# An order planned with later landings and later hand-overs, attention norms through PSUM, and the modulation's weights in the first ffn

## The chip, the cores and the metric

The kernel runs on one core of a Trainium2 chip. The metric is the device time in microseconds (us) of one execution. Three executions of the kernel before took 1523.7, 1526.34 and 1527.78 us; the median is 1526.34.

The engines are TensorE (PE: matmuls and transposes), VectorE (DVE), ScalarE (ACT), GpSimd (POOL) and SyncE (SP, which issues the loads).

## The reference

256 tokens of width 1024 go through two blocks. The first has two layers, and each layer a mixer and an ffn:

```
h    = rms_norm(x);  proj = h @ w_in[l]
o_a  = ga0*compressed_attn + ga1*selected_attn + ga2*banded_attn(window 512)
o_b  = silu(layer_norm(depthwise_conv31(a * sigmoid(g))))
o_c  = pool_mixer(c_in)
o_d  = banded_attn(window 128, sinks)            # exp(sink - m) joins the denominator
mix  = sum over b of sigmoid(h @ w_gate[l])_b * (o_b @ w_branch[l, b])
x    = x + rms_norm(mix @ w_o[l])
u    = depthwise_conv3(rms_norm(x) @ w_up);  gate, val = split(u)
x    = x + rms_norm((gelu(gate) * val) @ w_down)
```

In the compressed attention, 15 compressed keys for each of two groups, the probabilities are `softmax` over the masked scores, weighted by the gate `ga0`.

The second block takes the result and a condition c. Its modulation is `silu(c) @ w_mod + b_mod` (w_mod is 1024 x 6144), with a second product `silu(c_ctx) @ w_mod[:, :2048]` for a context of 256 tokens that has its own side computation. Shifts, scales and gates from it enter a mixer with attention and a state scan, and a mixture of 16 experts. Nothing in the first block needs the modulation.

## The kernel before

**Where the time goes, in order.** Mixer 0 runs from the start to about 335 us of the profile, ffn 0 to about 525, mixer 1 to about 815, and the rest is ffn 1 and the second block. Each mixer has a head (the in-projections, with the attentions, the 31-tap convolution on VectorE and the pool mixer beside them), then gates and branches (`gate`, `branch`: 16 products whose weights stream in), then w_o and its renorm.

**Matmuls.** Weights are loaded by SP in tiles of 512 KB (`wr_wr`). ACT rounds a tile to the PE's type (`wh_wh`); POOL, and sometimes VectorE, subtracts the two (`wl_wl` = wr - wh, both inputs in SBUF). Activations are split the same way (`hp_hTh`/`hp_hTl`, `bp_brh`/`bp_brl`), and PE does three matmuls for each product. Everything that PE writes, and some small work of the other engines, goes through eight PSUM banks, all named `ps_bank`.

**What sets the order.** The program is first recorded, not issued. A list scheduler (`run`, L374) then places the recorded instructions on the engines by estimated costs (`cost`, L240), hand-over latencies between engines (`lat`, L298) and a model of the DMA queue; `slack` (L327) works out priorities from the result, and `order` (L306) repeats this ten times and keeps the best. `emit` (L540) issues the instructions in that order, so every instruction in the profile has line L540 and is told apart by its names. Each engine executes its own instructions strictly in this order. What VectorE costs, how late a load is taken to land and how late a result is taken to reach another engine thus set what stands before what, and nothing else.

**The modulation** (`modulation`, L1756). w_mod comes in 96 tiles of 128x512 (`wm_wm`, 256 KB, two buffers), in groups of eight. A row of silu(c), 512 wide, is kept in a PSUM bank for a group, and one SCALAR_TENSOR_TENSOR on VectorE multiplies a tile by it and sums along the row. The first sixteen tiles of the order and the last sixteen are multiplied twice, once for c and once for c_ctx (into a scratch `wk_t2k`), and their groups hold two banks. The generator goes on only while `k.m_on` is set: before, from the first gate of a mixer (L1596) to the start of that layer's ffn (L1657), or to `conv_start` (L1456) in a mixer's head. Its results are first used by the second block, which starts with the w_o of layer 1.

**The attentions.** `attn` (L1085) makes scores, their row minimum `mx` (the scores are negated) and the exponentials with their row sums `sm`. `norm` (L1115) turns the sums into weights: with sinks it adds exp(mx - sinks), then takes the reciprocal `w`, multiplied by the gate where there is a weight, all on 8 columns in SBUF. There are 12 calls of it, four with sinks and eight with a weight. `cmp_attn` (L1300) is the compressed attention: two score matmul groups into one bank, mask, maximum, exponential and sum on VectorE and ACT, then reciprocal, weight and the product `wk_t1k`, which PE transposes. It runs beside the gates.

**ffn** (L1648). Four banks (`n.py`) hold the output sums during an ffn. Up-projections of 128x256 pairs take a bank each; `evac` reads it (three-tap convolution, ACT and VectorE), `act` and `sp` use the same bank for gelu and the split into `bp_brh` and `bp_brl`, after which it is free. `renorm` follows each w_o and each ffn: row sums of squares, a Newton iteration on 128x1 columns on VectorE (`wk_sm`, `wk_nw`, `wk_nwy`), the residual, transposes by PE.

## Time and profile before

| | |
|---|---|
| median of three executions | 1526.34 us |
| the profiled execution | 1523.77 us |
| its span, first to last instruction | 1521.6 us |
| mean granted TensorE clock | 0.984 |
| PE busy | 1437.5 us, 94% |
| VectorE, ACT, GpSimd busy | 69%, 65%, 64% |
| read from HBM | 287.13 MB, 189 GB/s over the span |
| w_mod loads issued, by place | 43 before layer 0's w_up, 7 in ffn 0's head, 37 in mixer 1's gates, 9 behind the first w_o load of layer 1 |

A time in the rows is in us from the start of the span. A duration in brackets is the time that the engine was idle before the instruction, with the instruction or load that ended the idle time. The granted clock (PEclk) is a fraction of full speed: 1.00 is 2.4 GHz and 0.50 is 1.2. In the windows an engine's entry is its busy time and its number of instructions.

### The profile page before, as it was taken

How to read it: one execution, taken by the hardware profiler on the slowest of the kernel's cores; microseconds unless marked ns; L12 is line 12 of the kernel's file. 1: busy time of each engine (PE TensorE's matmuls, PEld its weight loads, DVE VectorE, ACT ScalarE, POOL GpSimd, SP SyncE). 2: the span in 40 equal slices, each digit the busy share in tenths (PEclk: the TensorE clock that was granted, in tenths of full speed). 3: DMA queues.
4: the chain of work that ended last, by engine and by line, in shares of the span. 5: the costliest groups of instructions: out<-in, count | busy, mean ns of one | idle time of the engine just before them, and what ended most of it. 6: DMA issues, size and time to landing. Idle time of an engine off the chain costs nothing.

```text
span 1521.6 us, 23981 instructions
## 1 busy us (share of the span) xinstructions
PE 1437.5 (94%) x8276; PEld 1233.2 (81%) x8276; DVE 1050.8 (69%) x2412; ACT 983.9 (65%) x1773; POOL 971.1 (64%) x504
## 2 busy tenths in 40 slices
PE   8989998989999999899999999999999999899995
PEld 6967886769999798788777999999888778777773
DVE  5889765554333669985467843336888886889997
ACT  5878953556555577886356665556567697476773
POOL 6786587848777677947786677777647572332121
PEclk9999999999999999999999999999999999999998
DMA  8555478856555454637786555555534205358982
GB/s 315 167 172 166 143 263 266 271 195 207 183 189 183 133 193 136 204 127 257 256 273 220 190 182 191 182 186 169 158 116 134 88 29 175 112 180 302 343 291 89
DMA packets 91155, 290.35 MB, mean 191 GB/s; under 512 B 11409, under 2 KB 13713, under 8 KB 91026
## 3 DMA queue, kind: packets, MB, share of 16 engines
q1 hardware_dynamic: 91026, 288.74, 57.0%
q8 instruction: 67, 1.10, 0.3%
q14 instruction: 62, 0.51, 0.1%
HBM read 287.13 MB, written 1.05 MB: 189 GB/s over the span
## 4 chain that ended last, share of the span: by engine, by line
PE 70%; DVE 14%; DMA 8%; ACT 5%; issue 2%; POOL 1%; SPq 0%; DVEq 0%; ACTq 0%; POOLq 0%
PE ps_bank L540 70%; DMA wm_wm<-w_mod 7%; DVE wl_wl L540 3%; DVE wk_t2k L540 3%; DVE ps_bank L540 3%; ACT wh_wh L540 2%; DVE wm_wm L540 2%; ACT wk_t2k L540 1%; DVE wk_t4k L540 1%; DVE wk_sm L540 1%; ACT wk_t4k L540 1%; POOL wl_wl L540 1%; DVE wk_nw L540 0%; DMA wr_wr<-w_qd 0%; DVE cp_x L540 0%
## 5 line engine op out<-in xcount | busy, mean ns | idle before, releaser
L540 POOL TENSOR_TENSOR wl_wl<-wr_wr,wh_wh 128x1024 fp32r<-128x1024 f32 (+2 forms) x346 | 823.9, 2391 | 434.1 <-ACT wh_wh L540 405.2
L540 ACT ACTIVATE wh_wh<-wr_wr 128x1024 fp32r<-128x1024 f32 (+2 forms) x446 | 464.6, 1045 | 297.5 <-PE ps_bank L540 197.4
L540 PE MATMUL ps_bank<-hp_hTh,wh_wh 128*128 128x256 f32 x928 | 266.8, 288 | 0.8 <-DVE hp_hTl L540 0.8
L540 PE MATMUL ps_bank<-wh_wh,hp_hTh 128*128 128x512 f32 (+3 forms) x656 | 260.3, 398 | 4.2 <-ACT hp_hTh L540 2.2
L540 PE MATMUL ps_bank<-hp_hTh,wl_wl 128*128 128x256 f32 x928 | 263.1, 284 | 0.0
L540 PE MATMUL ps_bank<-hp_hTl,wh_wh 128*128 128x256 f32 x928 | 263.1, 284 | 0.0
L540 PE MATMUL ps_bank<-wl_wl,hp_hTh 128*128 128x512 f32 (+3 forms) x656 | 256.1, 391 | 4.1 <-DVE wl_wl L540 4.1
L540 PE MATMUL ps_bank<-wh_wh,hp_hTl 128*128 128x512 f32 (+3 forms) x656 | 254.5, 388 | 0.3 <-DVE hp_hTl L540 0.2
L540 PEld LDWEIGHTS ps_bank<-hp_hTh,wh_wh 128*128 128x128 f32 x928 | 178.3, 192 | 3.6 <-DVE hp_hTl L540 1.1
L540 DVE SCALAR_TENSOR_TENSOR wk_t2k<-ps_bank,cl_cols,wk_t2k 128x255 f32<-128x255 f32 (+1 forms) x176 | 84.7, 482 | 139.1 <-ACT wk_t2k L540 135.9
L540 PEld LDWEIGHTS ps_bank<-hp_hTl,wh_wh 128*128 128x128 f32 x928 | 178.4, 192 | 2.5 <-issue 1.2
L540 PEld LDWEIGHTS ps_bank<-hp_hTh,wl_wl 128*128 128x128 f32 x928 | 178.3, 192 | 0.0
L540 DVE TENSOR_TENSOR wl_wl<-wr_wr,wh_wh 128x1024 fp32r<-128x1024 f32 (+2 forms) x100 | 151.5, 1531 | 29.3 <-ACT wh_wh L540 28.9
L540 PE MATMUL ps_bank<-wh_wh,wk_t4k 128*128 128x512 f32 (+2 forms) x496 | 155.1, 384 | 1.4 <-ACT wk_t4k L540 1.1
L540 PEld LDWEIGHTS ps_bank<-wh_wh,hp_hTh 128*128 128x128 f32 x656 | 125.3, 191 | 32.3 <-ACT hp_hTh L540 4.3
L540 PEld LDWEIGHTS ps_bank<-wl_wl,hp_hTh 128*128 128x128 f32 x656 | 125.3, 191 | 31.1 <-DVE wl_wl L540 6.4
L540 PEld LDWEIGHTS ps_bank<-wh_wh,hp_hTl 128*128 128x128 f32 x656 | 124.9, 190 | 26.2 <-DVE hp_hTl L540 2.4
L540 DVE SCALAR_TENSOR_TENSOR wm_wm<-wm_wm,ps_bank 128x512 f32<-128x512 f32 x96 | 65.1, 686 | 71.0 <-DMA wm_wm<-w_mod 69.9
L540 DVE SCALAR_TENSOR_TENSOR ps_bank<-wk_cpad,pp_cwh,ps_bank 128x256 f32<-128x256 f32 x232 | 110.4, 486 | 4.5
L540 PEld LDWEIGHTS ps_bank<-wh_wh,wk_t4k 128*128 128x128 f32 x496 | 91.1, 188 | 19.5 <-ACT wk_t4k L540 1.6
L540 ACT ACTIVATE wk_t2k<-ps_bank 128x512 fp32r<-128x512 f32 (+6 forms) x156 | 81.3, 530 | 25.2 <-PE ps_bank L540 21.5
L540 PE MATMUL ps_bank<-wl_wl,wk_t4k 128*128 128x512 f32 (+2 forms) x248 | 94.3, 381 | 3.4 <-DVE wl_wl L540 3.4
(309 smaller groups left out, 2604.8 us busy)
## 6 DMA issues: line engine op xcount, KB each, us to landing
wr_wr<-w_up SPq DMA_DIRECT2D x88, 512.0 KB, 3.7
wr_wr<-w_gate SPq DMA_DIRECT2D x64, 512.0 KB, 4.4
wm_wm<-w_mod SPq DMA_DIRECT2D x96, 256.0 KB, 3.7
wr_wr<-w_down SPq DMA_DIRECT2D x44, 512.0 KB, 3.8
wr_wr<-w_gu SPq DMA_DIRECT2D x40, 512.0 KB, 5.6
wr_wr<-w_br SPq DMA_DIRECT2D x32, 512.0 KB, 5.0
wk_t4k<-w_gu SPq DMA_DIRECT2D x24, 512.0 KB, 7.0
wr_wr<-w_xbc SPq DMA_DIRECT2D x22, 512.0 KB, 4.4
```

Source lines behind the costliest of these rows:

```text
L540: getattr(getattr(r.nc, o.e), o.f)(*[real(x) for x in o.a], **{n: real(x) for n, x in o.kw.items()})
```

## The change

Four things change.

1. The planner's numbers. A VectorE instruction is taken to cost 0.075 + n/920 us instead of 0.069 + n/960; a result is taken to reach PE 0.5 us after its end instead of 0.26, and other engines but GpSimd 0.2 instead of 0.14 (L298); a load is taken to land 2.0 us after its transfer instead of 0.77. None of these is executed.
2. `norm` takes a PSUM bank. With sinks ACT copies `mx` into it, and the difference, exponential and sum read it there; with a weight the reciprocal is written to it. Each VectorE instruction with two inputs then has at most one in SBUF. Four ACTIVATEs are added in the program.
3. `cmp_attn` writes its reciprocals into free columns of the bank that holds its scores, and two SCALAR_TENSOR_TENSORs (gate and row factor in one) replace two TENSOR_TENSORs on SBUF.
4. The modulation is not switched on in mixer 0's gates any more, but at the start of ffn 0, and stays on until `conv_start` of mixer 1. It goes on in mixer 1's gates as before. SP's order now has 2 w_mod loads before layer 0's w_up, 55 in ffn 0, 17 in mixer 1's head and 22 in mixer 1's gates; none is behind the first w_o load of layer 1.

```diff
--- before.py
+++ after.py
@@ -265,7 +265,7 @@
                 n *= 6
             if o.f in ("tensor_scalar", "tensor_copy", "tensor_single_scalar") and not any(x.t.psum for x in vs):
                 n /= 2
-            return 0.069 + n / 960 + 0.06 * ptr, None
+            return 0.075 + n / 920 + 0.06 * ptr, None
         if o.f == "memset":
             return 0.035 + n / 1200, None
         return 0.148 + n / 464, None
@@ -301,7 +301,7 @@
             return {"tensor": 0.0, "vector": 0.127, "scalar": 0.143, "gpsimd": 0.1}.get(a.e, 0.0)
         if a.e == "tensor":
             return 0.2
-        return {"tensor": 0.26, "gpsimd": 0.165}.get(b.e, 0.14)
+        return {"tensor": 0.5, "gpsimd": 0.165}.get(b.e, 0.2)
 
     def order(r, after, rounds=1):
 
@@ -480,7 +480,7 @@
                 at[e] = s + o.cost
                 dma[1] = max(dma[1], s + 0.05) + 0.46
                 dma[0] = max(dma[0], dma[1] + 0.65) + max(0.07, o.kind / 1048576 * 2.91)
-                o.end = dma[0] + 0.77
+                o.end = dma[0] + 2.0
             else:
                 c = o.cost
                 if e == "scalar" and o.kind in (AF.Exp, AF.Tanh, AF.Gelu_apprx_tanh):
@@ -1113,15 +1113,19 @@
                 yield 2.5
 
             def norm(mx=mx, sm=sm, sinks=sinks, sbs=sbs, n=n, weight=weight):
+                sp = k.bank("aux")
                 if sinks is not None:
-                    e = k.t([128, 8], "sm8")
-                    nc.vector.tensor_tensor(e, mx, sinks, op=ALU.subtract)
+                    e = sp[:, :8]
+                    nc.scalar.activation(e, mx, AF.Copy)
+                    nc.vector.tensor_tensor(e, e, sinks, op=ALU.subtract)
                     nc.scalar.activation(e, e, AF.Exp)
-                    nc.vector.tensor_tensor(sm, sm, e, op=ALU.add)
+                    nc.vector.tensor_tensor(sm, e, sm, op=ALU.add)
                 w = k.t([128, 8], "sm8")
-                nc.vector.reciprocal(w, sm)
-                if weight is not None:
-                    nc.vector.tensor_tensor(w, w, weight, op=ALU.mult)
+                if weight is None:
+                    nc.vector.reciprocal(w, sm)
+                else:
+                    nc.vector.reciprocal(sp[:, 8:16], sm)
+                    nc.vector.tensor_tensor(w, sp[:, 8:16], weight, op=ALU.mult)
                 for j in range(4):
                     for g in range(2):
                         s = sbs[j][:, g, :n]
@@ -1339,12 +1343,13 @@
         nc.vector.tensor_tensor(pf, pf, mx[:, :, :, None].to_broadcast([128, 8, 2, 16]), op=ALU.subtract)
         nc.scalar.activation(pf, pf, AF.Exp, scale=0.125)
         nc.vector.tensor_reduce(sm, pf, AX.X, ALU.add)
-        rec = k.t([128, 8, 2], "sm16")
+        rec = ps.rearrange("p t j n -> p (t j) n")[:, :, 48:50]
         nc.vector.reciprocal(rec, sm)
         yield 2.5
         w = k.t([128, 2, 8], "sm16")
-        nc.vector.tensor_tensor(w, rec.rearrange("p (t j) g -> p t (j g)", t=2), ga[:, :, :8], op=ALU.mult)
-        nc.vector.tensor_tensor(w, w, k.c("rowv")[:, :, None].to_broadcast([128, 2, 8]), op=ALU.mult)
+        for tt in range(2):
+            nc.vector.scalar_tensor_tensor(w[:, tt].rearrange("p (j g) -> p j g", g=2), ps[:, tt, :, 48:50], k.c("rowv")[:, tt:tt + 1],
+                                           ga[:, tt, :8].rearrange("p (j g) -> p j g", g=2), op0=ALU.mult, op1=ALU.mult)
         sc = k.t([128, 2, 8, 16], "t1k")
         nc.vector.tensor_tensor(sc.rearrange("p t (j g) n -> p (t j) g n", g=2), pf,
                                 w.rearrange("p t (j g) -> p (t j) g", g=2)[:, :, :, None].to_broadcast([128, 8, 2, 16]), op=ALU.mult)
@@ -1593,7 +1598,7 @@
 
         yield k.share("gate")
         yield from gate(2, 0)
-        yield lambda: m_on(True)
+        yield lambda: m_on(l > 0)
         yield mix_start
         yield from branch(2, 0)
         yield from gate(2, 1)
@@ -1654,7 +1659,7 @@
             if l + 1 == L:
                 k.drain("R")
                 k.do_rest()
-            k.m_on = False
+            k.m_on = l == 0
             n.fw = k.col("fconvw").rearrange("p (m w) -> p m w", w=3)
             n.fb = k.col("fconvb")
             n.py = [[k.bank("mm"), k.bank("mm")], [k.bank("mm"), k.bank("po")]]
```

VectorE's order in mixer 0 at `cmp_attn`, from the w_mod tiles ahead of it to the product that PE transposes; `wm_wm` are w_mod's tiles, `cp_const` the mask, `wk_ga` the gate. Before:

```order
L540 TENSOR_TENSOR wl_wl_2783<-wr_wr_2649,wh_wh_2766 128x1024
L540 SCALAR_TENSOR_TENSOR wm_wm_2758,cp_mod_2309<-wm_wm_2758,ps_bank_2532 128x512
L540 SCALAR_TENSOR_TENSOR wm_wm_2778,cp_mod_2309<-wm_wm_2778,ps_bank_2532 128x512
L540 SCALAR_TENSOR_TENSOR wm_wm_2801,cp_mod_2309<-wm_wm_2801,ps_bank_2532 128x512
L540 TENSOR_TENSOR ps_bank_2824<-ps_bank_2824,cp_const_105 128x4x32 x2
L540 TENSOR_REDUCE wk_sm_0_2853<-ps_bank_2824 128x16
L540 TENSOR_TENSOR ps_bank_2824<-ps_bank_2824,wk_sm_0_2853 128x8x32
L540 SCALAR_TENSOR_TENSOR wm_wm_2816,cp_mod_2309<-wm_wm_2816,ps_bank_2532 128x512
L540 TENSOR_REDUCE wk_sm_1_2868<-ps_bank_2824 128x16
L540 RECIPROCAL wk_sm_2_2874<-wk_sm_1_2868 128x16
L540 TENSOR_TENSOR wk_sm_0_2882<-wk_sm_2_2874,wk_ga_424 128x16
L540 TENSOR_TENSOR wk_sm_0_2882<-wk_sm_0_2882,cp_const_105 128x16
```

The product `wk_t1k` is the next row there. The changed kernel, same engine and place, with the product:

```order
L540 TENSOR_TENSOR wl_wl_2675<-wr_wr_2571,wh_wh_2661 128x1024
L540 TENSOR_TENSOR ps_bank_2710<-ps_bank_2710,cp_const_98 128x4x32 x2
L540 TENSOR_REDUCE wk_sm_0_2735<-ps_bank_2710 128x16
L540 TENSOR_TENSOR ps_bank_2710<-ps_bank_2710,wk_sm_0_2735 128x8x32
L540 TENSOR_REDUCE wk_sm_1_2753<-ps_bank_2710 128x16
L540 RECIPROCAL ps_bank_2710<-wk_sm_1_2753 128x8x2
L540 SCALAR_TENSOR_TENSOR wk_sm_2_2763<-ps_bank_2710,cp_const_98,wk_ga_425 128x8 x2
L540 TENSOR_TENSOR wk_t1k_2768<-ps_bank_2710,wk_sm_2_2763 128x256
```

The four w_mod tiles are gone from the chain, and the reciprocal and the weights go through the bank.

VectorE's order in the renorm at ffn 0's end (`cp_x` is the residual, `wk_sm` and `wk_nw` the Newton iteration). Before:

```order
L540 SCALAR_TENSOR_TENSOR cp_x_73<-ps_bank_3818,wk_nwy_5540,cp_x_73 128x512
L540 SCALAR_TENSOR_TENSOR cp_x_73<-ps_bank_3822,wk_nwy_5540,cp_x_73 128x512
L540 TENSOR_SCALAR wk_sm_5565<-wk_sm_5555 128x1
L540 TENSOR_SCALAR wk_nw_5569<-wk_sm_5562,wk_sm_5565 128x1
L540 TENSOR_SCALAR wk_nw_5571<-wk_nw_5569 128x1
```

and in the changed kernel:

```order
L540 SCALAR_TENSOR_TENSOR cp_x_73<-ps_bank_3656,wk_nwy_5589,cp_x_73 128x512
L540 SCALAR_TENSOR_TENSOR cp_x_73<-ps_bank_3662,wk_nwy_5589,cp_x_73 128x512
L540 SCALAR_TENSOR_TENSOR wm_wm_5532,cp_mod_0_5150<-wm_wm_5532,ps_bank_5440 128x512
L540 TENSOR_SCALAR wk_sm_5616<-wk_sm_5609 128x1
L540 SCALAR_TENSOR_TENSOR wm_wm_5560,cp_mod_0_5150<-wm_wm_5560,ps_bank_5440 128x512
L540 TENSOR_SCALAR wk_nw_5621<-wk_sm_5612,wk_sm_5616 128x1
L540 TENSOR_SCALAR wk_nw_5627<-wk_nw_5621 128x1
```

Two w_mod tiles now stand inside this chain.

SP's order of loads in ffn 0, early in its up-projections. Before:

```order
L540 DMA wr_wr_3478<-w_up 128x1024
L540 DMA wr_wr_3506<-w_up 128x1024
L540 DMA wr_wr_3535<-w_down 128x1024
L540 DMA wr_wr_3569<-w_down 128x1024
L540 DMA wr_wr_3650<-w_up 128x1024
```

and in the changed kernel:

```order
L540 DMA wm_wm_3876<-w_mod 128x512
L540 DMA wr_wr_3881<-w_up 128x1024
L540 DMA wr_wr_3912<-w_up 128x1024
L540 DMA wm_wm_3920<-w_mod 128x512
L540 DMA wr_wr_3938<-w_up 128x1024
L540 DMA wm_wm_3952<-w_mod 128x512
L540 DMA wr_wr_3974<-w_up 128x1024
L540 DMA wm_wm_3997<-w_mod 128x512
L540 DMA wr_wr_4009<-w_down 128x1024
L540 DMA wm_wm_4032<-w_mod 128x512
```

About one load in two is now a w_mod tile.

## Rows read from the trace of the kernel before

**Rows 1.** PE's busy time, share of the span and instructions, from the page's first part.
```profile
PE 1437.5 (94%) x8276; PEld 1233.2 (81%) x8276; DVE 1050.8 (69%) x2412; ACT 983.9 (65%) x1773; POOL 971.1 (64%) x504
```

**Rows 2.** Windows in the gates, ffn 0, mixer 1's head: start:end, us, engines, PEclk, DMA, GB/s.
```profile
205.00:235.00 30.00, 30.00 (x133) 24.54 (x132) 17.71 (x47) 14.74 (x17) 27.27 (x12) 1.00 0.76 246
400.00:440.00 40.00, 40.00 (x286) 37.63 (x286) 15.64 (x31) 22.46 (x34) 28.84 (x12) 1.00 0.57 186
530.00:690.00 160.00, 154.13 (x908) 131.44 (x907) 137.20 (x383) 129.23 (x297) 109.32 (x60) 1.00 0.51 165
```

**Rows 3.** What PE waited for, 150 to 335 us: us in total, times, longest.
```profile
PE ps_bank L540 <- DVE wk_t1k L540: 6.3, 1, 6.3
PE ps_bank L540 <- DVE wk_nwy L540: 4.1, 1, 4.1
```

**Rows 4.** Timeline, mixer 0's `cmp_attn`: start, us, engine, operation, out<-in [idle before <-releaser].
```profile
250.39 0.69 DVE L540 SCALAR_TENSOR_TENSOR wm_wm<-wm_wm,ps_bank 128x512 f32<-128x512 f32 x1 [1.94 <-DMA wm_wm<-w_mod]
...
251.00 0.63 DVE L540 TENSOR_TENSOR ps_bank<-ps_bank,cp_const 128x128 f32<-128x128 f32 x2
...
254.80 0.66 PE L540 MATMUL ps_bank<-cp_ident,wk_t1k 128*128 128x128 f32 x2 [6.26 <-DVE wk_t1k L540]
```

**Rows 5.** Windows in which the granted clock was half: after two of the waits.
```profile
253.20:260.00 6.80, 5.20 (x21) 4.84 (x22) 3.37 (x10) 3.56 (x6) 3.71 (x2) 0.50 0.86 287
806.10:809.60 3.50, 3.29 (x13) 2.40 (x12) 3.14 (x9) 0.60 (x1) 3.23 (x2) 0.51 0.65 241
```

**Rows 6.** Timeline, mixer 1's `cmp_attn`.
```profile
759.73 0.63 DVE L540 TENSOR_TENSOR ps_bank<-ps_bank,cp_const 128x128 f32<-128x128 f32 x2
...
763.36 0.44 PE L540 MATMUL ps_bank<-cp_ident,wk_t1k 128*128 128x128 f32 x2 [1.57 <-DVE wk_t1k L540]
```

**Rows 7.** Timeline, the renorm at mixer 0's end.
```profile
316.52 0.20 ACT L540 ACTIVATION_READ_ACCUMULATOR wk_t4k<-ps_bank 128x1 f32 x1
...
317.45 0.69 DVE L540 SCALAR_TENSOR_TENSOR wm_wm<-wm_wm,ps_bank 128x512 f32<-128x512 f32 x1 [1.82 <-DMA wm_wm<-w_mod]
...
318.06 0.21 DVE L540 TENSOR_SCALAR wk_nw<-wk_sm,wk_sm 128x1 f32<-128x1 f32 x1
```

**Rows 8.** Timeline, the renorm at ffn 0's end.
```profile
521.71 1.49 PE L540 MATMUL ps_bank<-cp_ident,wk_t4k 128*128 128x128 f32 x8 [2.91 <-DVE wk_sm L540]
```

**Rows 9.** Timeline, mixer 1's gates: a subtraction on VectorE and its reader.
```profile
739.02 3.27 DVE L540 TENSOR_TENSOR wl_wl<-wr_wr,wh_wh 128x1024 fp32r<-128x1024 f32 x1
...
742.35 0.50 PE L540 MATMUL ps_bank<-wl_wl,bp_brh 128*128 128x512 f32 x1 [1.72 <-DVE wl_wl L540]
```

**Rows 10.** Timeline, ffn 0: the same subtraction, a bank's release, its next matmul.
```profile
400.20 1.22 DVE L540 TENSOR_TENSOR wl_wl<-wr_wr,wh_wh 128x1024 fp32r<-128x1024 f32 x1 [4.04 <-ACT wh_wh L540]
...
407.40 0.42 DVE L540 TENSOR_TENSOR bp_brl<-ps_bank,bp_brh 128x256 fp32r<-128x256 f32 x1
...
410.34 0.28 PE L540 MATMUL ps_bank<-hp_hTh,wh_wh 128*128 128x256 f32 x1
```

**Rows 11.** Timeline, the start of mixer 1's w_o.
```profile
800.40 3.42 DVE L540 TENSOR_TENSOR wl_wl<-wr_wr,wh_wh 128x1024 fp32r<-128x1024 f32 x1
...
805.82 0.86 PE L540 MATMUL ps_bank<-cp_ident,mp_mix 128*128 128x128 f32 x4 [1.28 <-POOL mp_mix L540]
```

**Rows 12.** VectorE's small instructions by form: xcount | busy us, mean ns | idle before.
```profile
L540 DVE TENSOR_TENSOR wk_sm<-wk_sm,wk_ga 128x8 f32<-128x8 f32 x8 | 4.7, 584 | 0.2
L540 DVE TENSOR_TENSOR wk_sm<-wk_sm,wk_sm 128x8 f32<-128x8 f32 x4 | 4.5, 1114 | 0.0
...
L540 DVE TENSOR_TENSOR ps_bank<-ps_bank,wk_nwy 128x8 f32<-128x8 f32 x8 | 1.4, 173 | 0.2
```

**Rows 13.** What PE waited for, 40 to 150 us, mixer 0's head.
```profile
PE ps_bank L540 <- DVE wk_sm L540: 1.2, 3, 0.8
```

**Rows 14.** The w_mod tiles: VectorE's waits for them (us, times), and their landing.
```profile
  DMA wm_wm<-w_mod: 95.6, 55
...
DMA to landing us min/median/max: 2.5/3.7/8.5
```


## The prediction

> **What bounds the kernel now.** I read the page's busy shares first. TensorE (PE) is busy for 1437.5 us, 94% of the span, and no other engine passes 69% [rows 1]. So an edit pays only where it ends a wait of PE, or where PE works at the lower of its two clock levels (1.2 instead of 2.4 GHz; the granted clock reads 0.50 there). Next I read the windows by stage, to know which stages have something to give. In the middle of the first ffn PE is busy 40.00 of 40.00 us, at clock 1.00 [rows 2]: nothing can be won there, only lost. The mixers do have waits. PE's list of waits for mixer 0 (150 to 335 us) has two large ones: 6.3 us for VectorE's `wk_t1k` and 4.1 us for VectorE's `wk_nwy` [rows 3]. The rest of the argument is about what VectorE does just ahead of such a hand-over.
>
> The timeline of mixer 0 shows the first. `cmp_attn` scores, masks, exponentiates and scales on VectorE, and PE then transposes the result, `wk_t1k`. In between VectorE executes SCALAR_TENSOR_TENSORs of `modulation`, one per w_mod tile, and it takes its instructions in order: one that waits for its tile holds up everything behind it. The one at 250.39 us had waited 1.94 us for its load, and the chain's mask follows it at 251.00; PE begins its transposes at 254.80 after a wait of 6.26 us [rows 4]. After that wait PE runs for 5.20 us at clock 0.50 [rows 5]. Mixer 1 has the same chain with one such tile: 3.63 us from the mask at 759.73 to PE's transposes at 763.36, and a wait of only 1.57 us [rows 6].
>
> **The change part by part.** Everything is summed against the profiled execution's own time, 1523.77 us (its span is 1521.6); the median of the three runs, 1526.34, is 2.57 above it, and I add that at the end.
>
> *Modulation leaves mixer 0's gates* (the `m_on` edits). In the order before, four w_mod tiles stand ahead of or inside `cmp_attn`'s chain; in the new order there is none, only one `wl_wl` ahead of it. The gates still to be multiplied cover it: between the score matmuls and the transposes PE's new order has 21 matmuls of 512 columns; PE does 133 such matmuls in 30.00 us of the gates [rows 2], 0.226 us each, so these are 4.7 us of cover, against a chain of 3.6 us by mixer 1's rows. So the wait of 6.26 us goes, and with it the cause of the low clock that followed it: 5.20 us of work at half speed would have taken 2.6. **Term 1: -8.9 us.** If the `wl_wl` ahead is a slow one (3.27 us, see below), 2.1 us of waiting come back: bounds -8.9 to -6.3. I take -8.9, because in the new order that subtraction is queued before the score matmuls end.
>
> *The renorms.* At mixer 0's end a w_mod tile that waited 1.82 us stood ahead of the row statistics: the sum of squares was there at 316.72 us (316.52 plus 0.20) and VectorE took it up at 318.06 [rows 7]. It moves away: -1.3. At ffn 0's end the reverse happens: PE already waits 2.91 us for VectorE's `wk_sm` chain there [rows 8], and the new order puts two tiles into the middle of that chain and two right behind. Two in front of what PE waits for cost 2 x 0.69 = 1.4 if their loads are in, and up to 1.9 more if one is not [rows 4]: +1.5 (bounds 0 to +3.3). **Term 2: +0.2.**
>
> *Fewer tiles late in mixer 1* (37 w_mod loads in its gates and 9 behind the first w_o before; 22 and none after, since 55 go through ffn 0 and 17 through mixer 1's head). In the gates PE waits 1.72 us for a `wl_wl` made by VectorE, which took 3.27 us for an instruction that elsewhere takes 1.22 [rows 9, 10], and 1.57 us for `wk_t1k` [rows 6]. A w_mod tile stands ahead of the second. I take less than half of these 3.29 us: **Term 3: -1.3** (0 to -3.3). At w_o's start PE waits 1.28 us for `mp_mix`, behind a `wl_wl` of 3.42 us and a w_mod tile on VectorE [rows 11], and then runs 3.29 us of work at clock 0.51 [rows 5], which is 1.6 us lost. The tile goes; whether the slow `wl_wl` does is open. Half: **Term 4: -1.5** (0 to -2.9).
>
> *The norm edits.* Small VectorE instructions on 8 columns take 584 and 1114 ns when both inputs are in SBUF, and 173 ns when one is in a PSUM bank [rows 12]. The edit turns them into the second kind: 8 x (584 - 173) + 4 x (1114 - 173) = 7.1 us of VectorE's time, spread over eight places. It adds four ACTIVATEs on 8 columns, off PE's path. On PE's side only the waits for `wk_sm` can shrink: 1.2 us in three waits in mixer 0's head [rows 13], and the same line in mixer 1's head. **Term 5: -1** (0 to -2.4). GpSimd subtracts one SBUF tile from another for most of its time; the long values beside that fit the Trainium skill, page "SBUF — State Buffer", section "Who interferes with whom": a VectorE instruction with two SBUF inputs contends with a GpSimd instruction that reads SBUF, and with one at most it does not. By that rule the edit gains all of the 7.1 us on VectorE; what PE gets of it is still bounded by the waits.
>
> *Modulation in ffn 0 and mixer 1's head.* This is the new burden. 72 tiles (55 + 17) at 0.69 us, the first 16 twice, are 61 us more of VectorE. In ffn 0 VectorE is busy for 15.64 of 40 us and DMA for 0.57 [rows 2]; there is room. What is tight is the order: a tile that is not there holds the up-projection's evacuation, and with it a PSUM bank. In ffn 0 four banks hold the sums and two the rows of c while the first 16 tiles run, so two are left for the ups. In the present trace a bank is released at 407.82 (the instruction at 407.40 plus its 0.42) and next written by PE at 410.34: 2.5 us of slack [rows 10]. The mean wait of VectorE for a w_mod tile now is 95.6 / 55 = 1.7 us, and the median landing 3.7 us after issue [rows 14]. In the new order a w_mod load is issued among the w_up loads, two buffers ahead. 1.7 is inside 2.5; some tiles will not be. In mixer 1's head VectorE is busy 137.20 of 160 us already [rows 2], and 17 tiles add 12. **Term 6: +1.5** (0 to +10: the upper end is six tiles overrunning the slack by what the 3.7 us leave of it, 1.2 us each, and 2.6 us for one drop of the clock).
>
> *The planner's numbers* (later landings, later hand-overs to PE, longer VectorE instructions). They cost nothing to execute; they re-sort. PE's order is almost the same (8291 rows before, 8289 after), so the second block, behind the modulation, keeps its waits in kind. **Term 7: 0** (-4 to +4, some four small waits of about 1 us won or lost).
>
> The sum: -8.9 + 0.2 - 1.3 - 1.5 - 1.0 + 1.5 + 0 = **-11.0 us**: 1523.77 - 11.0 = 1512.8, and 1515.3 with the 2.57 of the median.
>
> **The rivals.** About 0.3%, 4.6 us, is what a measurement of this kernel can tell from no change: faster is below 1521.7, slower above 1530.9.
>
> *The slow subtractions stay.* VectorE's `wl_wl` at 3.27 and 3.42 us run beside GpSimd's own `wl_wl`, not because of modulation; nothing in the diff parts the two. Then terms 3 and 4 are nought and term 1 loses its 2.1 us: -8.9 + 2.1 + 0.2 - 1.0 + 1.5 = -6.1, the median 1520. For it: the order still has `wl_wl` on VectorE at each of these places. Against it: 1.22 us for another copy of the instruction, so the slow form is not the rule. The page just named says that the lock holds for the whole instruction, and the row of 3.27 beside 1.22 agrees.
>
> *The order does better than the terms.* With hand-overs to PE reckoned later, VectorE's products for PE come earlier everywhere, and the short waits outside the mixers shrink too: terms 3 to 5 at their ends (-8.6) and -4 of term 7, with nothing for term 6: -8.9 + 0.2 - 8.6 - 4 = -21, the median 1505. Against it: a scheduler that is told of later landings must also give up something, and ffn 0 can only lose.
>
> *No change.* The wait moves: `cmp_attn`'s gain is eaten by the renorm of ffn 0 at its upper end (+3.3) and by term 6 at +8.5, as the price of tiles in a stretch where PE had none: -11.0 + 1.8 + 7.0 = -2.2, the median 1524. For it: ffn 0 has no slack on PE at all [rows 2].
>
> *Slower.* The mechanism is the bank in ffn 0. If w_mod tiles land later than 2.5 us behind the point at which VectorE comes to them, PE stops in each of the eight up-projections that run beside the two doubled groups, and after each stop it works at half clock for some 3.3 us, as behind the wait of 1.28 [rows 5, 11], which loses 1.6. With 1.2 us of stop each: 8 x (1.2 + 1.6) = 22, against the gain of 12.5 of the terms without term 6: +10, the median 1536. It decides where the mean wait for a tile passes 2.5 us instead of 1.7.
>
> **How the numbers follow.** Forecast (1508 to 1520) 0.45; slow subtractions stay (1518 to 1522) 0.15; better order (1502 to 1508) 0.12; no change (1521 to 1528) 0.15; slower (1530 to 1545) 0.13. Faster: 0.45 + 0.12 + most of 0.15 and a fifth of the no-change case = 0.74; same 0.14; slower 0.12. The range 1504 to 1528 leaves out the slower case and the best part of the better order.
>
> **What will show it.** Right: in mixer 0 no wait of PE for `wk_t1k` above 1.5 us and no stretch at clock 0.50 behind it; VectorE waits for w_mod of 2 us at most on the mean in ffn 0, with PE still at 40 of 40 us there; the renorm of ffn 0 with a wait of 3 to 5 us instead of 2.91; `reciprocal` and weight instructions in PSUM at under 0.2 us. Wrong: PE waits for a bank (a release by `bp_brl` or `wk_t2k`) in ffn 0, new stretches at half clock, or VectorE at 95% and more in mixer 1's head, with the conv's sums late.

## The result, and the profile after

The changed kernel takes 1503.08 us (median of four runs, 1501.16 to 1504.87) against 1525.02 for the kernel before (four runs, 1516.28 to 1527.78, the three shown earlier among them). The ratio is 0.9876, with a 95% interval of 0.9853 to 0.9898: a gain of 18.9 us, between 15.6 and 22.4. The four runs of the kernel before lie high: in the three groups of runs made later its medians are 1520.68, 1520.06 and 1522.56 us, against which 1503.08 would be a gain of 17.0 to 19.5. The forecast was -11.0, a time of 1515.3 in a range of 1504 to 1528. The sign is right and the gain is larger. The plain median lies 0.9 us under the range; the ratio, put on the median that the forecast started from, gives 1507.4, inside it.

The first part of the page of the changed kernel:

```profile
span 1501.6 us, 23962 instructions
...
PE 1433.5 (95%) x8276; PEld 1234.6 (82%) x8276; DVE 1035.5 (69%) x2412; ACT 980.7 (65%) x1777; POOL 976.0 (65%) x504
```

PE is busy for 4.0 us less than in [rows 1], and the span is 20.0 us shorter: 16.0 us of the gain are idle time of PE. What PE waited for in the whole span, largest first (us in total, times, longest):

```profile
PE ps_bank L540 <- DVE wk_t4k L540: 8.8, 6, 4.2
PE ps_bank L540 <- DVE wl_wl L540: 7.5, 7, 2.2
PE ps_bank L540 <- DVE wk_t2k L540: 4.7, 5, 1.9
...
PE ps_bank L540 <- DVE wk_t1k L540: 0.6, 1, 0.6
...
PE ps_bank L540 <- DVE wk_nwy L540: 0.2, 1, 0.2
```

Of the two waits of [rows 3], the one for `wk_t1k` is gone from mixer 0; 0.6 us in one wait is left in the whole span. The one for `wk_nwy` has only changed its name. In the renorm at mixer 0's end PE waits 3.75 us, now until `wk_nw`, and 0.15 until `wk_nwy`, against 4.1 before:

```profile
315.90 0.63 PE L540 MATMUL ps_bank<-cp_ident,wk_t4k 128*128 128x128 f32 x4 [3.75 <-DVE wk_nw L540]
316.68 0.63 PE L540 MATMUL ps_bank<-cp_ident,wk_t4k 128*128 128x128 f32 x4 [0.15 <-DVE wk_nwy L540]
```

The longest wait, 4.2 us for `wk_t4k`, is at ffn 0's end, where [rows 8] have 2.91.

To see where the time went I take nine stretches between the same PE instructions of each trace: from the start to the first gate matmul on `bp_brh` (head 0), to the first transpose of `mp_mix` (gates 0), to ffn 0's first up-projection (w_o 0), to its last (ffn 0), to the last matmul with `pp_poolw` (head 1), to the last transpose of `mp_mix` (gates 1), to the first projection of the scan's inputs (ffn 1), to their last (scan in), and to the last matmul (rest). In us, for the kernel before, the same kernel once more (experiment 12) and the changed one:

| | head 0 | gates 0 | w_o 0 | ffn 0 | head 1 | gates 1 | ffn 1 | scan in | rest |
|---|---|---|---|---|---|---|---|---|---|
| before | 148.6 | 147.4 | 45.5 | 160.0 | 154.2 | 153.7 | 291.9 | 49.0 | 355.4 |
| before, again | 147.8 | 147.2 | 45.5 | 160.0 | 154.2 | 152.8 | 291.8 | 49.0 | 355.4 |
| changed | 149.0 | 138.4 | 44.6 | 160.0 | 153.9 | 146.4 | 288.5 | 43.5 | 361.4 |

Gates 0 gives 9.0 us, gates 1 7.3, the scan's inputs 5.5, ffn 1 3.4; the rest takes 6.0 back. Head 1 holds the renorm at ffn 0's end. The two traces of the kernel before agree within 0.9 us in every stretch; both executions had a mean granted clock of 0.984, so they do not show what a stretch takes in an execution with a lower one (the last section comes back to this).

The timeline of the changed kernel at mixer 0's `cmp_attn`, to be held against [rows 4]:

```profile
242.48 1.94 PE L540 MATMUL ps_bank<-wk_cm,wk_t4k 128*128 128x48 f32 x16
...
244.45 0.63 DVE L540 TENSOR_TENSOR ps_bank<-ps_bank,cp_const 128x128 f32<-128x128 f32 x2 [5.55 <-PE ps_bank L540]
...
247.63 0.36 DVE L540 SCALAR_TENSOR_TENSOR wk_sm<-ps_bank,cp_const,wk_ga 128x8 f32<-128x8 f32 x2
...
248.02 0.42 DVE L540 TENSOR_TENSOR wk_t1k<-ps_bank,wk_sm 128x256 f32<-128x256 f32 x1
...
249.18 0.38 PE L540 MATMUL ps_bank<-cp_ident,wk_t1k 128*128 128x128 f32 x2
```

The mask now follows PE's score matmuls at once, VectorE having waited for PE and not for a load; the product is done at 248.44, and PE's transposes at 249.18 show no wait. The windows of the changed kernel (ffn 0; the renorm at its end; one in the second block):

```profile
332.00:492.00 160.00, 159.85 (x1155) 151.37 (x1154) 103.28 (x268) 97.92 (x150) 129.59 (x56) 1.00 0.85 280
511.80:518.60 6.80, 5.17 (x15) 3.77 (x16) 6.70 (x19) 4.65 (x9) 6.68 (x4) 0.50 0.60 196
1293.50:1314.00 20.50, 17.02 (x78) 15.95 (x77) 15.21 (x59) 6.55 (x12) 0.89 (x1) 0.50 0.30 101
```

In ffn 0 VectorE is busy for 103.28 us instead of 61.62 (the same 160 us before) and DMA for 0.85 of the time, and PE loses nothing. Behind ffn 0's end, and in the second block at 1293.5 us, there are stretches at half clock. The same view of the whole "rest", of the changed kernel and then of the kernel before:

```profile
1124.70:1485.70 361.00, 341.02 (x1674) 274.30 (x1672) 310.57 (x522) 249.53 (x423) 137.94 (x74) 0.96 0.51 178
1150.30:1505.70 355.40, 335.03 (x1677) 268.01 (x1675) 308.12 (x518) 250.36 (x424) 137.89 (x75) 0.99 0.52 180
```

PE is idle for 20.0 us in the one and 20.4 in the other. The 6.0 us that the rest takes back are longer busy time of PE, at a mean clock of 0.96 instead of 0.99.

### The profile page after: what moved, and what is told of

Read it like the earlier page. It is cut to its first block, busy times and chain, and to the rows that moved or that the text cites. A ratio compares the mean times of both kernels' runs of the same rounds, so it can differ in the third digit from the quotient of the medians.

```text
span 1501.6 us, 23962 instructions
## 1 busy us (share of the span) xinstructions
PE 1433.5 (95%) x8276; PEld 1234.6 (82%) x8276; DVE 1035.5 (69%) x2412; ACT 980.7 (65%) x1777; POOL 976.0 (65%) x504
## 4 chain that ended last, share of the span: by engine, by line
PE 82%; DVE 8%; ACT 4%; issue 3%; POOL 1%; DMA 1%; SPq 0%; ACTq 0%; POOLq 0%; DVEq 0%
PE ps_bank L540 82%; DVE ps_bank L540 2%; ACT wh_wh L540 1%; DVE wk_t2k L540 1%; DVE wk_t4k L540 1%; DVE wl_wl L540 1%; POOL wl_wl L540 1%; ACT wk_t2k L540 1%; ACT wk_t4k L540 1%; DVE wk_sm L540 1%; DMA wr_wr<-w_qd 1%; DVE wk_nw L540 0%; ACT hp_hTh L540 0%; ACT ps_bank L540 0%; DVE cp_x L540 0%
## 5 line engine op out<-in xcount | busy, mean ns | idle before, releaser
L540 DVE TENSOR_TENSOR wl_wl<-wr_wr,wh_wh 128x1024 fp32r<-128x1024 f32 (+2 forms) x100 | 152.8, 1543 | 72.3 <-ACT wh_wh L540 70.5
L540 ACT ACTIVATE wk_t2k<-wk_t2k,wk_sm 128x128 f32<-128x128 f32 (+2 forms) x200 | 84.8, 457 | 10.0 <-DVE wk_sm L540 9.5
```

What stands on the lines that cost most here:

```text
L540: getattr(getattr(r.nc, o.e), o.f)(*[real(x) for x in o.a], **{n: real(x) for n, x in o.kw.items()})
```

## Experiments

Each was run in the same way: the kernel, its profile, and its time against the kernel before on the same chip (experiment 12 has one time). The stretches are those of one profiled execution, which need not be the median: in experiments 1 and 2 it took 7.5 and 3.6 us more than the median, in experiment 5 4.0 less. Ratios are to the kernel before of that group of runs (1520.68, 1520.06 and 1522.56 us). The edits are parts of the change: the switches (`m_on`), the norms (`norm` and `cmp_attn` through PSUM), and the planner's three kinds of numbers (landing, hand-over, VectorE's cost).

**1. The switches alone.**

```diff
-        yield lambda: m_on(True)
+        yield lambda: m_on(l > 0)
-            k.m_on = False
+            k.m_on = l == 0
```

> The kernel before with the modulation's two switch edits alone (off in mixer 0's gates, on from ffn 0); planner's numbers and norms as before. Theory A (where the tiles stand does it): the stretch from mixer 0's gates to its w_o loses about 9 us as in the changed kernel, PE's wait for wk_t1k there is under 1.5 us, the renorm at ffn 0's end grows by 1 to 2 us, mixer 1's gates lose 2 to 6; the time is 1507 to 1514 against 1525. Theory B (the planner's later landings and hand-overs do it): 1518 to 1524, with a wait of PE for wk_t1k above 3 us left in one mixer.

Measured: 1521.74 us, ratio 1.0015 (0.9983 to 1.0047). Gates 0 takes 138.4 us as in the changed kernel, so theory A is right on that place, and theory B, whose range holds the time, is not: no wait for `wk_t1k` above 1.1 us is left anywhere in the span. But ffn 0 takes 166.2 instead of 160.0 and head 1 159.9 instead of 154.2, and the whole gain is eaten. The renorm at ffn 0's end, which was to grow, has a wait of 2.91 us as before. What PE waited for in ffn 0 here, 336 to 502 us, and then the place itself in the timeline:

```profile
PE ps_bank L540 <- DVE wm_wm L540: 2.2, 1, 2.2
PE ps_bank L540 <- DVE bp_brl L540: 1.9, 2, 1.0
```

```profile
378.81 0.69 DVE L540 SCALAR_TENSOR_TENSOR wk_t2k<-wm_wm,ps_bank 128x512 f32<-128x512 f32 x1 [1.01 <-DMA wm_wm<-w_mod]
...
379.54 0.69 DVE L540 SCALAR_TENSOR_TENSOR wm_wm<-wm_wm,ps_bank 128x512 f32<-128x512 f32 x1
...
380.16 0.43 DVE L540 TENSOR_TENSOR ps_bank<-ps_bank,wk_t2k 128x256 f32<-128x256 f32 x1
...
380.29 0.39 PE L540 MATMUL ps_bank<-hp_hTh,wh_wh 128*128 128x256 f32 x1 [2.19 <-DVE wm_wm L540]
...
381.03 0.42 DVE L540 TENSOR_TENSOR bp_brl<-ps_bank,bp_brh 128x256 fp32r<-128x256 f32 x1 [0.45 <-ACT bp_brh L540]
```

The two products of one w_mod tile, the sixteenth (for c_ctx and for c), stand on VectorE ahead of a product that ends in `bp_brl`. The first waited 1.01 us for the tile at 378.81; the second, at 379.54, is the last that reads a bank with a row, and PE has waited 2.19 us for it at 380.29. Then 3.4 us of PE's work run at half clock:

```profile
336.00:502.00 166.00, 161.96 (x1154) 152.34 (x1153) 106.20 (x272) 96.15 (x148) 128.50 (x54) 0.99 0.81 271
380.80:384.20 3.40, 3.40 (x18) 3.40 (x18) 2.09 (x5) 1.60 (x3) 2.18 (x1) 0.50 0.58 185
```

PE's idle time in ffn 0 is 166.00 - 161.96 = 4.0 us, and half of 3.40 is 1.7: 5.7 of the 6.2 us. This is the mechanism of the rival named "slower" in the prediction, met at three places instead of eight and with half clock behind one of them.

**2. The norms alone** (`norm` and `cmp_attn` as in the diff of the change, nothing else).

> The kernel before with the norm and compressed-attention edits alone (through PSUM); modulation and planner's numbers as before. Theory A: about 1524 (1520 to 1527); the weights' instructions on 8 columns fall from 584 and 1114 ns to under 200, and PE keeps a wait for wk_t1k of 4 to 7 us in mixer 0. Theory B: the same. A third theory (VectorE's time on locked small instructions is what PE waits for): 1515 to 1518.

Measured: 1525.8 us, ratio 1.0027 (1.0006 to 1.0048). The instructions got as short as expected; VectorE's forms on 8 columns in this kernel:

```profile
L540 DVE TENSOR_TENSOR wk_sm<-ps_bank,wk_ga 128x8 f32<-128x8 f32 x8 | 1.3, 165 | 0.2
...
L540 DVE TENSOR_TENSOR wk_sm<-ps_bank,wk_sm 128x8 f32<-128x8 f32 x4 | 0.6, 160 | 0.3 <-ACT ps_bank L540 0.2
```

584 and 1114 ns in [rows 12] have become 165 and 160. PE got nothing of it: head 0 takes 148.7 us (148.6 before), PE's wait for `wk_t1k` in mixer 0 is there with 7.4 us, and w_o 0 takes 51.6 instead of 45.5: PE is idle there for 2.0 us more, with a wait of 3.8 us for `hp_hTl` that the kernel before doesn't have, and its mean clock is 0.87 instead of 0.96. The third theory falls.

**3. The planner's numbers alone.**

```diff
-            return 0.069 + n / 960 + 0.06 * ptr, None
+            return 0.075 + n / 920 + 0.06 * ptr, None
-        return {"tensor": 0.26, "gpsimd": 0.165}.get(b.e, 0.14)
+        return {"tensor": 0.5, "gpsimd": 0.165}.get(b.e, 0.2)
-                o.end = dma[0] + 0.77
+                o.end = dma[0] + 2.0
```

> The kernel before with the planner's four numbers alone. The order of VectorE still has w_mod tiles ahead of and inside the compressed attention's chain in both mixers. Theory A: PE's wait for wk_t1k in mixer 0 stays at 4 to 7 us, and the time is 1518 to 1530. Theory B: later reckoned landings put enough matmuls between, the wait falls under 2 us, and the time is 1505 to 1514.

Measured: 1512.6 us, ratio 0.9945 (0.9925 to 0.9965). Theory A, on which the forecast stood, expected the wait for `wk_t1k` to stay; it is gone, and gates 0 takes 139.9 us, with the modulation still in these gates. So numbers that are not executed gave some 8 us by themselves.

**4. The change without the switches** (norms and planner's numbers).

> The changed kernel with the modulation's switches put back (on in mixer 0's gates, off in ffn 0); planner's numbers and norms as changed. Theory A: the 9 us of mixer 0 come back as a wait of PE for wk_t1k and half clock behind it, those of mixer 1's gates too; 1515 to 1524. Theory B: within 5 us of the changed kernel, 1500 to 1508.

Measured: 1509.77 us, ratio 0.992 (0.9888 to 0.9952), beside 0.9876 (0.9853 to 0.9898) of the whole change; the intervals overlap a little. Neither theory had it: the 9 us of gates 0 did not come back (138.2), those of gates 1 did (154.6 us against 146.4), by a wait of 2.4 us for `mp_mix` and 6.8 us at half clock around it.

After these four runs theory A is refuted as an account of the whole. In mixer 0 the switches (1) and the planner's numbers (3, 4) each end the wait for `wk_t1k` without the other. The next four take single numbers out of the change, to see which it is.

**5. Landing as before.**

```diff
-                o.end = dma[0] + 2.0
+                o.end = dma[0] + 0.77
```

> The changed kernel with the landing of a load reckoned as before (0.77 instead of 2.0 us); all else as changed. Theory C (the later landing is what makes modulation harmless in ffn 0): ffn 0 and the renorm behind it cost 5 to 12 us more than in the changed kernel, VectorE waits for w_mod tiles in ffn 0 while PE waits for a bank; 1509 to 1518. Theory D (the later hand-over to PE does nearly all of it): within 4 us of the changed kernel, 1499 to 1507, and PE without a wait above 1 us in ffn 0.

Measured: 1516.76 us, ratio 0.9976 (0.9958 to 0.9993). ffn 0 takes 165.4 us and head 1 160.1, as in experiment 1. PE's waits in ffn 0 (330 to 495.3 us), and VectorE's for w_mod in the same window:

```profile
PE ps_bank L540 <- DVE wm_wm L540: 2.3, 1, 2.3
PE ps_bank L540 <- POOL wl_wl L540: 0.9, 1, 0.9
PE ps_bank L540 <- DVE wl_wl L540: 0.7, 1, 0.7
```

```profile
  DMA wm_wm<-w_mod: 45.1, 33
...
DMA to landing us min/median/max: 2.5/4.3/6.5
```

The same two views of the changed kernel (332 to 492 us):

```profile
PE ps_bank L540 <- POOL wl_wl L540: 0.2, 1, 0.2
```

```profile
  DMA wm_wm<-w_mod: 29.4, 26
...
DMA to landing us min/median/max: 2.5/4.6/6.1
```

This is theory C's result. VectorE waits 29.4 us for w_mod even in the changed kernel, 1.1 us a time against 1.4 here; what is different is that PE's list has no wait for a bank released behind such a tile.

**6. Hand-overs as before.**

```diff
-        return {"tensor": 0.5, "gpsimd": 0.165}.get(b.e, 0.2)
+        return {"tensor": 0.26, "gpsimd": 0.165}.get(b.e, 0.14)
```

> The changed kernel with the hand-overs reckoned as before (0.26 us to PE and 0.14 to others instead of 0.5 and 0.2). Theory C: the short waits of PE in the mixers and in the second block return, worth 3 to 8 us, ffn 0 stays at nothing; 1506 to 1511. Theory D: the gain of the planner's numbers is gone; 1514 to 1522, with the compressed attention's wait still cured by the switches.

Measured: 1503.28 us, ratio 0.9909 (0.988 to 0.9938). That cannot be told from the whole change. ffn 0 takes 159.9 us. Theory D falls; theory C expected 3 to 8 us of short waits to return, and they did not either. The hand-overs are worth nothing that these runs can see. In ffn 0 VectorE waits 38.3 us for w_mod in 34 times here, as much as in experiment 1 (38.2 in 32), and PE loses nothing where it lost 6 us there.

**7. VectorE's cost as before.**

```diff
-            return 0.075 + n / 920 + 0.06 * ptr, None
+            return 0.069 + n / 960 + 0.06 * ptr, None
```

> The changed kernel with VectorE's instructions reckoned as before (0.069 + n/960 us). Theories C and D alike: within 4 us of the changed kernel, 1499 to 1507. If every change of the planner's numbers shuffles the order by chance (theory E), it can be anywhere from 1497 to 1515.

Measured: 1506.32 us, ratio 0.9926 (0.9902 to 0.9949): in the range that was expected, which theory E's range holds as well. The interval just misses that of the whole change (0.9853 to 0.9898). Single stretches move all the same: ffn 1 294.1 instead of 288.5, the rest 356.7 instead of 361.4.

**8. Switches and norms, the planner as before.**

> The kernel before with the modulation's switches and the norms through PSUM, but the planner's numbers as before. If the parts add up by what the switches alone (+1 us) and the norms alone (+4) did: 1522 to 1528, with waits for w_mod in ffn 0. If the norms help as they do on top of the planner's numbers (-3 us): 1514 to 1519.

Measured: 1518.09 us, ratio 0.9979 (0.9959 to 0.9999): under the first expectation and in the second. ffn 0 166.3, head 1 159.3: with the landing as before the modulation in ffn 0 costs 5 to 6 us there, a third time.

**9. The landing alone** (the one line of experiment 5, the other way, on the kernel before).

> The kernel before with one number changed: a load is reckoned to land 2.0 us after its transfer instead of 0.77. Theory C (the landing number does the planner's part): most of what all the planner's numbers did alone, 1509 to 1515, with PE's wait for wk_t1k in mixer 0 gone although w_mod tiles stay in the gates. Theory E (every change of a number shuffles by chance): anywhere from 1508 to 1528.

Measured: 1511.74 us, ratio 0.9932 (0.9906 to 0.9958). One number does what the planner's three do together. The place in mixer 0, in the timeline of this kernel:

```profile
243.60 1.94 PE L540 MATMUL ps_bank<-wk_cm,wk_t4k 128*128 128x48 f32 x16
...
245.57 0.64 DVE L540 TENSOR_TENSOR ps_bank<-ps_bank,cp_const 128x128 f32<-128x128 f32 x2 [4.33 <-PE ps_bank L540]
...
247.04 0.68 DVE L540 SCALAR_TENSOR_TENSOR wm_wm<-wm_wm,ps_bank 128x512 f32<-128x512 f32 x1
...
248.81 0.42 DVE L540 TENSOR_TENSOR wk_t1k<-ps_bank,wk_sm 128x256 f32<-128x256 f32 x1
...
250.07 0.38 PE L540 MATMUL ps_bank<-cp_ident,wk_t1k 128*128 128x128 f32 x2
```

No waiting for a load is shown up to the product at 248.81, and PE's transposes at 250.07 show no wait. But the tiles do not stand where they did. In the kernel before, three of them and a `wl_wl` stand between PE's score matmuls and the mask of [rows 4]:

```profile
241.90 1.94 PE L540 MATMUL ps_bank<-wk_cm,wk_t4k 128*128 128x48 f32 x16
...
245.19 0.67 DVE L540 SCALAR_TENSOR_TENSOR wm_wm<-wm_wm,ps_bank 128x512 f32<-128x512 f32 x1
...
247.75 0.69 DVE L540 SCALAR_TENSOR_TENSOR wm_wm<-wm_wm,ps_bank 128x512 f32<-128x512 f32 x1 [1.88 <-DMA wm_wm<-w_mod]
```

The mask starts 7.2 us after the end of the score matmuls there, and 3.8 us of that are the waits of 1.88 and 1.94 us for tiles. In experiment 9 none stands there and the mask follows at once; one tile is left inside the chain, and the next one that is late stands behind the product:

```profile
251.24 0.69 DVE L540 SCALAR_TENSOR_TENSOR wm_wm<-wm_wm,ps_bank 128x512 f32<-128x512 f32 x1 [1.40 <-DMA wm_wm<-w_mod]
```

Over the whole kernel VectorE still waits 75.8 us for w_mod in 49 times, against 95.6 in 55 [rows 14]. So the number did not make the loads come in time; it moved what stands behind them.

**10. The landing and the switches.**

> The kernel before with the later landing and the modulation's switches, nothing else (norms, hand-overs and VectorE's cost as before). Theory C: ffn 0 takes 160.0 us from its first to its last up-projection as before, not 166; 1501 to 1509, as the whole change. If the norms through PSUM are needed too: 1509 to 1514.

Measured: 1508.75 us, ratio 0.9902 (0.987 to 0.9934). That cannot be told from the whole change. ffn 0 takes 162.2 us, not 160.0: the expectation of that stretch was missed by 2.2, 1.2 of it by waits for `bp_brl` (0.8 us) and a `wl_wl` (0.4).

**11. A still later landing** (3.0 us), the hand-overs as before.

> The changed kernel with a still later landing (3.0 us) and the hand-overs as before. Theory C: once the loads are early enough for the slack nothing more is won; 1499 to 1508, ffn 0 at 160.0 us. If waits for loads still cost in the rest: 1493 to 1499. If loads reckoned too late take buffers from each other: above 1508.

Measured: 1515.85 us, ratio 0.9957 (0.9937 to 0.9977). None of the first two: more is worse. ffn 0 stays good at 159.7 us, but w_o 0 takes 49.0, since PE waits longer at mixer 0's renorm than it does in the kernel before, and ffn 1 takes 296.4. PE's row there:

```profile
316.77 2.32 PE L540 MATMUL ps_bank<-cp_ident,wk_t4k 128*128 128x128 f32 x8 [7.17 <-DVE wk_sm L540]
```

VectorE's rows of this trace hold no w_mod tile in that place. Ahead of the product that PE waits for (315.88) stand three instructions on 512 columns for the residual of `cp_x` (313.27 to 315.41); in the changed kernel the residual stands behind that product (317.25 behind 315.01). So the order of the renorm itself differs. Whether that makes the whole 7.17 us, and whether the loads' buffers have a part in it, was not tested.

**12. The kernel before, once more.**

> The kernel before once more, for a second trace: which of its stretches differ from one execution to the next. If mixer 1's gates and the second block's first part are 5 us shorter here too, the gain seen there in nearly every variant is no effect of an edit; if they take the same time as in the first trace to 1 us, it is one of the order.

Measured: 1521.98 us. The stretches are in the table of the result. PE's row of mixer 0's transposes has 6.92 us where [rows 4] have 6.26, and gates 1 and the scan's inputs take 152.8 and 49.0 us: that is the first trace to 1 us, so the gain seen there in the variants goes with the order.

All variants by stretch, in us:

| | gates 0 | ffn 0 | head 1 | gates 1 | scan in | rest | ratio |
|---|---|---|---|---|---|---|---|
| before | 147.4 | 160.0 | 154.2 | 153.7 | 49.0 | 355.4 | 1 |
| changed | 138.4 | 160.0 | 153.9 | 146.4 | 43.5 | 361.4 | 0.9876 |
| 1 switches | 138.4 | 166.2 | 159.9 | 149.5 | 44.3 | 360.7 | 1.0015 |
| 2 norms | 147.9 | 159.5 | 155.5 | 151.8 | 47.5 | 356.1 | 1.0027 |
| 3 planner | 139.9 | 160.3 | 153.7 | 149.6 | 43.2 | 360.6 | 0.9945 |
| 4 no switches | 138.2 | 159.9 | 149.7 | 154.6 | 43.1 | 361.6 | 0.992 |
| 5 no landing | 138.6 | 165.4 | 160.1 | 145.7 | 43.1 | 360.1 | 0.9976 |
| 6 no hand-over | 138.5 | 159.9 | 155.3 | 146.5 | 43.2 | 361.7 | 0.9909 |
| 7 no cost | 138.6 | 160.2 | 155.1 | 145.9 | 43.4 | 356.7 | 0.9926 |
| 8 no planner | 138.4 | 166.3 | 159.3 | 147.1 | 44.4 | 358.0 | 0.9979 |
| 9 landing | 138.4 | 159.9 | 158.6 | 147.8 | 43.9 | 356.6 | 0.9932 |
| 10 landing, switches | 138.5 | 162.2 | 156.6 | 146.7 | 43.0 | 357.1 | 0.9902 |
| 11 landing 3.0 | 138.5 | 159.7 | 152.0 | 151.6 | 43.3 | 359.0 | 0.9957 |

Read down the columns. Gates 0 is 147 to 148 us in the kernel before and with the norms alone, 138 to 140 as soon as the switches or the landing are changed: either is enough, and they do not add. ffn 0 is 165 to 166 where the modulation runs in it with the landing as before (1, 5, 8), and 160 to 162 in all others. Gates 1 is 145.7 to 147.1 in six of the seven variants that have the switches and something of the planner or the norms (11 is the seventh, 151.6), and 147.8 to 154.6 elsewhere. The scan's inputs are 43 to 44 in all but the kernel before and the norms alone.

The ratios part by the landing. The seven orders planned with 2.0 us have 0.9876 to 0.9945, the five with 0.77, the kernel before among them, 0.9976 to 1.0027, and the one with 3.0 has 0.9957. That speaks against theory E as the cause: an edit that re-sorts by chance would not be expected to part them so.

## Why the prediction was right, and where it was not

**Term 1** (mixer 0's `cmp_attn`, -8.9): gates 0 measured -9.0, with the wait and the half clock behind it gone. The size is right, and so is the cause as far as the place goes: the tiles that held up the mask are gone from it in every variant that has the gain. That it takes the switches to move them is wrong: the landing alone moves them behind the product (experiment 9). The upper bound does not follow from its own term: with the 2.1 us of a slow `wl_wl` back it is -6.8, not -6.3.

**Term 2** (renorms, +0.2): half of it is right. In the renorm at mixer 0's end the w_mod tile is gone, but PE's wait is 3.9 us (3.75 and 0.15) instead of 4.1, so 0.2 to 0.3 us came of the 1.3 forecast. In the kernel before PE was at w_o's matmuls until 321.2, for 3.1 us after VectorE had taken up the row statistics of [rows 7] at 318.06, and so most of what VectorE lost there was covered. PE's rows there, before:

```profile
320.81 0.39 PE L540 MATMUL ps_bank<-wh_wh,hp_hTl 128*128 128x512 f32 x1
...
325.35 2.12 PE L540 MATMUL ps_bank<-cp_ident,wk_t4k 128*128 128x128 f32 x8 [4.15 <-DVE wk_nwy L540]
```

The stretch w_o 0 gave 0.9, with short waits elsewhere in it. At ffn 0's end PE's wait is 4.19 us instead of the 2.91 of [rows 8], +1.3 of the +1.5 forecast; the half clock there lasts 6.8 us instead of 3.4, which the term left out. PE's row there in the changed kernel:

```profile
513.25 1.97 PE L540 MATMUL ps_bank<-cp_ident,wk_t4k 128*128 128x128 f32 x8 [4.19 <-DVE wk_t4k L540]
```

**Terms 3 and 4** (mixer 1's gates and w_o, -2.8 together): mis-sized. Gates 1 measured -7.3 (-6.4 against the second trace of the kernel before). I halved each wait because the slow `wl_wl` of [rows 9, 11] might stay; all of them went. PE's list for 684 to 800 us of the changed kernel has one line:

```profile
PE ps_bank L540 <- ACT hp_hTh L540: 0.8, 1, 0.8
```

The ends that I had set (-3.3 and -2.9) come to -6.2. With them goes the half clock behind the wait for `mp_mix` [rows 5, 11], which was in the upper end. The rival "the slow subtractions stay" is refuted here: VectorE's `wl_wl` take 1.23 to 2.41 us in this stretch, and 3.42 at the most in the kernel before.

**Term 5** (norms, -1): not seen. The instructions became as short as [rows 12] said: 165 ns where two inputs in SBUF took 584. This agrees with the Trainium skill, page "SBUF — State Buffer", section "Who interferes with whom", by which a VectorE instruction with at most one input in SBUF does not contend with GpSimd. Alone they did not make the kernel faster (1.0027), and head 0 did not change. On the planner's numbers, 3 and 4 differ by 0.0025 with intervals that overlap, and so do 1 and 8 (1.0015 and 0.9979), so it stays open whether they give anything there.

**Term 6** (ffn 0 and head 1, +1.5): ffn 0 measured 0.0 and head 1 -0.3. That the value was near is luck, since the working behind it does not hold: with the switches alone (experiment 1) the two stretches lose 6.2 and 5.7 us, more than the upper bound of 10. I compared the mean wait for a tile, 1.7 us, with the 2.5 us for which a bank stood free [rows 10, 14]. By that measure experiments 1 and 5 should be like the changed kernel: their mean waits in ffn 0 are 38.2 / 32 = 1.2 and 45.1 / 33 = 1.4 us, the changed kernel's is 29.4 / 26 = 1.1. They lose 5 to 6 us, and it loses none. What goes with the loss is where the tile stands: in 1 and 5 PE waits 2.2 and 2.3 us for a bank that a w_mod product lets go, and in the changed kernel for none.

**Term 7** (planner's numbers, 0) is the step that failed. "They cost nothing to execute; they re-sort", I wrote, and priced the re-sorting as chance, -4 to +4. One of the numbers, the landing, gives a ratio of 0.9932 alone, and it is also what keeps term 6 at nothing: with it back, the change is worth 0.9976. It could have been read in the trace before: [rows 14] have a median landing of 3.7 us for a w_mod tile, and the planner's own formula, which I had, places it at 0.05 + 0.46 + 0.65 + 0.73 + 0.77 = 2.66 us after issue on a free queue, or 3.89 with the new number. A plan that takes its loads to be there a microsecond before they are puts VectorE in front of a tile that has not come, with work for PE behind it; I saw these waits (95.6 us in 55 times) and costed them as a property of the modulation instead of the plan. By stretches the change gave 9 us more than forecast (20.0 of the span against 11.0), 4.5 of them in gates 1 and 2.9 behind it; the terms 3 and 4 and this one are not told apart there, since the landing alone takes 5.9 us off gates 1 (147.8). The chances of the second rival, "the order does better than the terms", at 1505, should have been the larger for it; it came nearest in time. Its reason, later hand-overs, was wrong (experiment 6); the landing does it.

In the second block the sum of changes is small (from gates 1's end to the last matmul -3.4 + -5.5 + 6.0 = -2.9 us, inside term 7's bounds), made of parts that are larger. The scan's inputs had a wait of 3.02 us in the order before, with 6.8 us at half clock around it, and lose both in nearly every new order; no single number was found that does it. One sign of being wrong did show: there are new stretches at half clock, above all the one at 1293.5 us.

**What stays open.** What the switches add on top of the rest: 0.9876 against 0.992, with intervals that overlap a little, with gates 1 as the place (146.4 against 154.6 us). And the rest of the second block: 360 to 362 us in six of the variants, 355 to 359 in the six others and in the kernel before. PE's idle time there is no longer in the changed kernel (20.0 against 20.4), so it is the clock that differs; what in those orders lowers it is not shown. VectorE's cost in the plan goes with it in most of them, but experiment 1, with the cost as before, has 360.7. No version was found that is faster than the changed kernel; the ones without its hand-overs (6) or with landing and switches alone (10) are as fast within the intervals.

## What to carry to other kernels

Where a planner sets the order, its model of a load's landing is a lever as strong as moving work: compare it with the landing in the trace, under the traffic of that stage, before work is moved into another stage. Nearest to the trace is not always best: 3.0 us places a w_mod tile at 4.89 us after issue, close to that kernel's median of 4.7, and was slower than 2.0. A late load costs what is queued behind the instruction that waits for it, so look at whether a release that PE needs stands there, not at the mean wait. And since any edit re-sorts such a kernel, compare it stretch by stretch: one order repeated within 1 us in two executions at the same mean clock, and stretches moved by 5 between orders.

## What was not expected of the hardware

The half clock in the second block lasted far longer than the wait ahead of it: 20.50 us from 1293.5 in the changed kernel, during which PE was busy for 17.02 (windows above), behind a wait of 1.84 us for `cp_x` and with four more of 0.69 to 1.26 us inside. At full speed that work would take half the 17.02, so this stretch alone loses 8.5 us. It is not in this trace alone: that of experiment 1 has 20.5 us at half clock around the same place (from 1319.4), and the kernel before has 6.8 (from 1328.4).

The two profiled executions of the kernel before took 1523.77 and 1521.98 us, and their stretches agree within 0.9 us. Over 26 runs the same kernel took from 1512.48 to 1528.42 us. In these runs the spread goes with the granted clock: the mean clock of the fastest of the 26 is 0.988, that of the slowest 0.981, and 0.007 of 1520 us is an estimated 10.6 of the 15.9 us between them. In which stretch the clock is lost in the slower runs, these two traces do not show.
